# One core, three stacked blocks in float32: modulation sums by transposes, a joint compression of keys and values, a gMLP bias on VectorE and mLSTM maxima in float32r

## The chip, the core and the metric

The kernel runs on one NeuronCore of one Trainium2 chip. The metric is device time of one execution in microseconds (us). Matrix products run on TensorE (PE in the profile, its weight loads PEld), elementwise work on VectorE (DVE) and ScalarE (ACT), a little on GpSimd (POOL), and transfers are issued by SyncE (SP).

## The reference, cut to what matters

Three blocks follow each other on a sequence of 512 tokens of width 1024: an HGRN2 mixer with a gated convolution, a hybrid of gMLP, mLSTM and sparse attention (NSA) with an MLP, and a mixer of gated delta rule and RWKV-7 with a gated feed-forward part. The change touches four pieces of them:

```python
m = jax.nn.silu(cvec) @ w + b                      # modulation vectors, 1024 -> 3 or 6 times 1024

def compress_blocks(kv, pe, w1, w2):               # once for keys, once for values
    n_cmp = (S - CMP_BLOCK) // CMP_STRIDE + 1      # 31 blocks of 32 tokens, every 16
    idx = jnp.arange(n_cmp)[:, None] * CMP_STRIDE + jnp.arange(CMP_BLOCK)[None, :]
    blocks = kv[:, idx] + pe[:, None, :]
    blocks = blocks.transpose(0, 3, 1, 2, 4).reshape(B, G, n_cmp, CMP_BLOCK * dh)
    return jax.nn.gelu(blocks @ w1) @ w2

# gmlp_mixer: the bias is per group and token of a chunk
mixed = jnp.einsum('gts,bcsgd->bctgd', w, v) + bs.T[:, :, None]
return u * mixed.reshape(B, S, GM_W)

# mlstm_chunk_step: the running maximum m of each head and token enters two exponentials
s = jnp.einsum('bhtd,bhsd->bhts', q, k) * jnp.exp(d - m[..., None])
h = num / jnp.maximum(jnp.abs(den), jnp.exp(-m))[..., None]
```

## The kernel before, in words

Activations lie feature-major, 128 features on the partitions and 512 tokens along the row. Large products are done three times in float32r, with weights and activations split in a high and a low part (`mm3`, L320 to 327): high by high, high by low, low by high. `weight` (L303) loads 512 KB of weights into one of two raw buffers on SP's queue, ScalarE makes the high part (L310), VectorE the low part (L312). A projection is 24 such matmuls of 512 columns into one of three PSUM banks of tag "pj".

A planner in the framework orders the instructions: each has a priority (its place in the program, moved by `ahead`), and an engine is given what is ready by the planner's own durations. So instructions of one step lie between those of others, and the order on each engine is fixed before the run; at run time each engine takes its queue in that order.

The pieces that the change touches:

- `ada_later` (L483 to 501) makes 512 modulation values per step. VectorE sums eight weighted tiles of 128 by 512 into `ada_acc` (L492, L494). The sum over the 128 partitions is then taken by four matmuls with a quarter of `ada_acc` as the stationary operand and one column of ones as the moving one (L497), into a bank of tag "ad", of which there is one; VectorE adds the bias (L500). In float32 such a matmul has two records in the profile, so a step has eight. There are 32 steps: 12 in the loop over HGRN heads, 8 in the NSA steps, 12 in the MLP of block 2. The NSA steps use the same "ad" bank for gate projections.
- `small2` (L1119 to 1172) makes the mLSTM gate rows: scans on VectorE, a transpose (L1162), then eight ScalarE copies that put minus the running maximum and minus the total into rows 0 to 3 and 32 to 35 of `s_nmu` (L1170, L1171).
- `mlstm` (L1174) broadcasts, for each of four heads, one of those rows over 128 partitions by a matmul with a selecting matrix of four rows: twice before the scores (L1218, L1219; L1220 adds a mask to the second) and once after them (L1241). They are float32 of 512 columns, two records each.
- `nsa` (L1293 to 1321) first compresses keys, then values: project (24 matmuls), copy the result into `ns_st` in two shifts (L1302, L1303, ScalarE), 16 float32 matmuls with 64 columns of `ns_w` stationary and 3 times 31 strided columns of `ns_st` moving (L1306), a gelu, and a second small product (L1316, L1320).
- `gmlp` (L1476 to 1520): for each of four groups and four chunks, one product of 128 columns (L1513) and one product with a single row of ones that adds the bias (L1514) into the same bank; VectorE multiplies by `gm_u` (L1515).

Of the kernel before, what the change touches and what calls it, by code (L numbers as in the profile page):

```python
# [10 lines left out]
F32 = mybir.dt.float32  # L11
# [220 lines left out]
def dview(t, off, dims):  # L232

    return bass.AP(tensor=t.tensor, offset=t.offset + off, ap=[list(t.ap[0])] + [list(d) for d in dims])


class K:
# [245 lines left out]
    def ada_later(self, w, cond, groups, bias, out):  # L483

        def step(gi, grp):
# [9 lines left out]
            col = self.bank("ad", [P, 4])  # L495
            for b in range(4):
                nc.tensor.matmul(col[:, b:b + 1], acc[:, 128 * b:128 * b + 128], self.c("ones")[:, 0:1],  # L497
                                 start=True, stop=True)
            cs = slice(4 * gi, 4 * gi + 4)
            nc.vector.tensor_tensor(out[:, cs, 0], col, bias[:, cs], op=ALU.add)  # L500
# [618 lines left out]
    def small2(self, pl, pn):  # L1119
# [27 lines left out]
        L = pl.tile([P, S], F32, name="s2_L")  # L1147
# [17 lines left out]
        nn = pl.tile([36, S], F32, name="s2_nmu")  # L1165
# [6 lines left out]
        return gT, (acol, nmu, nm)  # L1172

    def mlstm(self, pl, pq, rows, ypair):  # L1174
# [4 lines left out]
        acol, nmu, nm = rows  # L1179
# [31 lines left out]
        for h in range(4):  # L1211
# [4 lines left out]
            sel, selm = [self.c("sel4")[a:a + 4, 128 * h:128 * h + 128] for a in (0, 32)]  # L1216
# [24 lines left out]
            mm(bm, selm, nm, start=True, stop=True)  # L1241
# [27 lines left out]
    def nsa(self, pn, gT, ypair, fill):  # L1269
# [18 lines left out]
        with tc_pool("x2_cmp") as pc:  # L1288
            for x, n in enumerate("kv"):
                st = pc.tile([P, 3, S], F32, name="ns_st", bufs=2)  # L1290
                pe = pn.tile([P, 16], F32, tag="pe", name="ns_pe")
                nc.sync.dma_start(pe, I["nsa_pe_" + n])
                w1 = pc.tile([P, 16, 64], F32, name="ns_w1", bufs=2)  # L1293
                nc.sync.dma_start(w1, I["nsa_phi_%s1" % n])
                w2 = pn.tile([64, 64], F32, tag="w2", name="ns_w2")
                nc.sync.dma_start(w2, I["nsa_phi_%s2" % n])
                nc.vector.memset(st[:, 2, :], 0.0)
                nc.vector.tensor_copy(dview(st[:, 2, :], 0, [[2, 16]]), pe)
                acc = self.proj_h(W[24 + x])
                for g in range(2):  # L1300
                    gs = slice(64 * g, 64 * g + 64)
                    nc.scalar.copy(st[0:64, g, :], acc[gs])  # L1302
                    nc.scalar.copy(st[64:128, g, 0:S - 1], acc[gs, 1:S])  # L1303
                hid = self.bank("mx", [64, 3, 31])
                for i in range(16):
                    mm(hid, w1[:, i, :], dview(st[:, :, :], 2 * i, [[S, 3], [16, 31]]), start=i == 0, stop=i == 15)  # L1306
                z, o = tmp("ns_z", [64, 2, 31]), tmp("ns_zo", [64, 2, 31])
# [886 lines left out]
```

## Time and profile before

| | |
|---|---|
| median of 3 runs (lowest, highest) | 3445.26 us (3436.17, 3450.95) |
| the profiled execution's own time | 3448.05 us |
| its span | 3446.3 us |
| PE, PEld, DVE, ACT busy share of the span | 96%, 77%, 70%, 52% |
| mean granted TensorE clock, share of full | 0.979 |
| HBM traffic over the span | 96 GB/s |

The profile is one execution. A row of the timeline gives the start in us from the span's start, the time to the end of the last instruction merged into it, engine, line, operation, the tile written and those read, shapes, and how many instructions; in brackets the idle time of the engine before it and what ended it. Because matmuls overlap, what one takes of TensorE is read from the distance of one start to the next, not from its duration. [...]

### The profile page before, as it was taken

How to read it: one execution, taken by the hardware profiler on the slowest of the kernel's cores; microseconds unless marked ns; L12 is line 12 of the kernel's file. 1: busy time of each engine (PE TensorE's matmuls, PEld its weight loads, DVE VectorE, ACT ScalarE, POOL GpSimd, SP SyncE). 2: the span in 40 equal slices, each digit the busy share in tenths (PEclk: the TensorE clock that was granted, in tenths of full speed). 3: DMA queues.
4: the chain of work that ended last, by engine and by line, in shares of the span. 5: the costliest groups of instructions: out<-in, count | busy, mean ns of one | idle time of the engine just before them, and what ended most of it. 6: DMA issues, size and time to landing. Idle time of an engine off the chain costs nothing.

```text
span 3446.3 us, 50617 instructions
## 1 busy us (share of the span) xinstructions
PE 3313.8 (96%) x20168; PEld 2647.7 (77%) x20168; DVE 2422.0 (70%) x3873; ACT 1808.1 (52%) x3020; POOL 123.6 (4%) x56
## 2 busy tenths in 40 slices
PE   7999999999799999999999999999999999999998
PEld 5888888888577777776787777878766767778886
DVE  7697767877789988667656456553777887655545
ACT  5566556566554556645445443333566665444434
POOL 0000000000032240000000000000000000000000
PEclk9999999999899999999999999999999999999999
DMA  6223333321122122334321235552311121322322
GB/s 226 87 95 97 103 95 104 100 85 60 44 68 68 62 69 97 123 101 126 107 84 59 84 120 180 179 164 98 105 57 52 52 66 62 120 89 95 98 93 85
DMA packets 113696, 332.43 MB, mean 96 GB/s; under 512 B 13170, under 2 KB 13810, under 8 KB 112819
## 3 DMA queue, kind: packets, MB, share of 16 engines
q1 hardware_dynamic: 113202, 328.41, 29.3%
q8 instruction: 158, 2.59, 0.3%
q0 software_dynamic: 256, 0.79, 0.1%
q14 instruction: 80, 0.65, 0.1%
HBM read 319.18 MB, written 9.96 MB: 96 GB/s over the span
## 4 chain that ended last, share of the span: by engine, by line
PE 76%; DVE 15%; ACT 4%; issue 2%; DMA 2%; SPq 0%; POOL 0%; DVEq 0%; ACTq 0%
PE ps_pj L326 19%; PE ps_pj L325 19%; PE ps_pj L327 19%; DVE w_lo L312 2%; DMA ada_raw<-ada_w 2%; PE ps_o L1444 1%; DVE iv_m L1817 1%; ACT w_hi L310 1%; PE ps_ad L497 1%; PE ps_mx L326 1%; DVE iv_xd L1818 1%; DVE cv_ul L318 1%; PE ps_mx L724 1%; DVE ada_acc L494 1%; PE ps_mx L327 1%
## 5 line engine op out<-in xcount | busy, mean ns | idle before, releaser
L325 PE MATMUL ps_pj<-hh,w_hi 128*128 128x512 f32 x2344 | 939.0, 402 | 20.0 <-ACT hh L397 18.9
L326 PE MATMUL ps_pj<-hl,w_hi 128*128 128x512 f32 x2344 | 934.0, 399 | 0.0
L327 PE MATMUL ps_pj<-hh,w_lo 128*128 128x512 f32 x2344 | 933.2, 399 | 0.0
L310 ACT CAST w_hi<-w_raw 128x1024 fp32r<-128x1024 f32 (+1 forms) x435 | 454.7, 1045 | 758.0 <-PE ps_pj L326 653.4
L312 DVE TENSOR_TENSOR w_lo<-w_raw,w_hi 128x1024 fp32r<-128x1024 f32 (+1 forms) x387 | 470.1, 1216 | 309.3 <-ACT w_hi L310 301.9
L325 PEld LDWEIGHTS ps_pj<-hh,w_hi 128*128 128x128 f32 x2344 | 445.5, 190 | 129.5 <-ACT hh L397 24.5
L326 PEld LDWEIGHTS ps_pj<-hl,w_hi 128*128 128x128 f32 x2344 | 445.3, 190 | 101.3 <-issue 11.8
L327 PEld LDWEIGHTS ps_pj<-hh,w_lo 128*128 128x128 f32 x2344 | 445.1, 190 | 100.8 <-issue 11.1
L494 DVE SCALAR_TENSOR_TENSOR ada_acc<-ada_raw,sv_t_c,ada_acc 128x512 f32<-128x512 f32 x224 | 167.3, 747 | 57.7 <-DMA ada_raw<-ada_w 56.3
L968 DVE SCALAR_TENSOR_TENSOR xT<-ps_pj,ad,xT 128x512 f32<-128x512 f32 x128 | 95.4, 748 | 153.6 <-PE ps_pj L327 153.0
L312 POOL TENSOR_TENSOR w_lo<-w_raw,w_hi 128x1024 fp32r<-128x1024 f32 x48 | 121.1, 2522 | 1176.0 <-ACT w_hi L310 1176.0
L910 DVE SCALAR_TENSOR_TENSOR ps_mx<-cv_ut,vec,ps_mx 128x448 f32<-128x448 f32 (+3 forms) x192 | 128.1, 668 | 1.9 <-PE ps_mx L327 1.0
L910 DVE SCALAR_TENSOR_TENSOR ps_ad<-cv_ut,vec,ps_ad 128x480 f32<-128x480 f32 (+2 forms) x192 | 128.4, 669 | 1.6 <-ACT ps_ad L899 0.5
L325 PE MATMUL ps_pj<-w_hi,hh 128*128 128x256 f32 x416 | 120.4, 290 | 0.8 <-ACT hh L397 0.7
L327 PE MATMUL ps_pj<-w_hi,hl 128*128 128x256 f32 x416 | 118.7, 287 | 2.5 <-DVE hl L398 2.5
L326 PE MATMUL ps_pj<-w_lo,hh 128*128 128x256 f32 x416 | 121.0, 292 | 0.0
L326 PE MATMUL ps_pj<-m_yl,w_hi 128*128 128x512 f32 x256 | 99.8, 390 | 0.0
L327 PE MATMUL ps_pj<-m_yh,w_lo 128*128 128x512 f32 x256 | 99.6, 389 | 0.0
L325 PE MATMUL ps_pj<-m_yh,w_hi 128*128 128x512 f32 x256 | 99.6, 389 | 0.0
L327 PEld LDWEIGHTS ps_pj<-w_hi,hl 128*128 128x128 f32 x416 | 80.7, 195 | 3.9 <-DVE hl L398 3.2
L325 PEld LDWEIGHTS ps_pj<-w_hi,hh 128*128 128x128 f32 x416 | 80.8, 194 | 3.1 <-issue 1.4
L326 PEld LDWEIGHTS ps_pj<-w_lo,hh 128*128 128x128 f32 x416 | 80.8, 194 | 1.9 <-issue 1.1
(783 smaller groups left out, 6430.2 us busy)
## 6 DMA issues: line engine op xcount, KB each, us to landing
ada_raw<-ada_w SPq DMA_DIRECT2D x288, 256.0 KB, 3.0
w_raw<-w_in SPq DMA_DIRECT2D x97, 512.0 KB, 3.7
w_raw<-hgrn_w_in SPq DMA_DIRECT2D x64, 512.0 KB, 3.7
w_raw<-w_mlp SPq DMA_DIRECT2D x64, 512.0 KB, 3.7
w_raw<-conv_w_in SPq DMA_DIRECT2D x48, 512.0 KB, 3.6
w_raw<-w_ffn_in SPq DMA_DIRECT2D x44, 512.0 KB, 3.5
w_raw<-hgrn_w_v SPq DMA_DIRECT2D x16, 512.0 KB, 3.7
w_raw<-hgrn_w_out SPq DMA_DIRECT2D x16, 512.0 KB, 3.7
```

The source lines that it names most:

```text
L310: nc.scalar.copy(hi, raw)
L312: (nc.gpsimd if self.on_pool else nc.vector).tensor_tensor(lo, raw, hi.bitcast(F32), op=ALU.subtract)
L318: self.nc.vector.tensor_tensor(lo, src, hi.bitcast(F32), op=ALU.subtract)
L325: mm(out, wh, xh, start=first, stop=False)
L326: mm(out, wh, xl, start=False, stop=False)
L327: mm(out, wl, xh, start=False, stop=last)
L494: nc.vector.scalar_tensor_tensor(acc, raw, cond[:, k:k + 1], acc, op0=ALU.mult, op1=ALU.add)
L497: nc.tensor.matmul(col[:, b:b + 1], acc[:, 128 * b:128 * b + 128], self.c("ones")[:, 0:1], start=True, stop=True)
L724: mm(up[:, 128 * j:128 * j + 128], kT[:, d, j, :], vx[:, j, hs], start=True, stop=True)
L910: stt(o, x, tap(j), o, op0=ALU.mult, op1=ALU.add)
L968: self.nc.vector.scalar_tensor_tensor(self.xT[:, m, :], acc, gate[:, m:m + 1], self.xT[:, m, :], op0=ALU.mult, op1=ALU.add)
L1444: mm(out[64 * g:64 * g + 64, 128 * s:], vt[:, s, 128 * b + 64 * g:128 * b + 64 * g + 64], pts[g][:, c:c + S - 128 * s], start=b == 0 and s ...
```

## The change

- The modulation sum: four transposes into a whole bank of 4 by 128 columns, a VectorE reduction over the 128 columns, and the bias added in place, instead of four matmuls with a column of ones.
- Compression: keys and values share one input tile `ns_st` of 2 by 3 by 512 and one weight tile `ns_w` whose 128 columns are 64 of keys and 64 of values. One run of 16 matmuls has 186 moving columns and computes both; the halves that mix keys with weights of values are not used. There is one gelu of 128 rows instead of two of 64.
- mLSTM: the rows are split in a float32r high and low part in one tile of 36 rows (a cleared tile is copied in first, on VectorE; ScalarE writes the high rows, VectorE the low rows), and the selecting matmul takes all 36 rows in float32r, one record each, with one column of a small tile repeated 128 times as the stationary operand. `s2_L` and the unsplit rows move to a pool of five rotating buffers.
- gMLP: the row of biases is loaded to all partitions, VectorE adds it to the product from PSUM (`gm_z`) and multiplies by `gm_u` in a second instruction. The matmuls with one row go.

```diff
--- before.py
+++ after.py
@@ -492,12 +492,12 @@
                     nc.vector.tensor_scalar(acc, raw, cond[:, k:k + 1], None, op0=ALU.mult)
                 else:
                     nc.vector.scalar_tensor_tensor(acc, raw, cond[:, k:k + 1], acc, op0=ALU.mult, op1=ALU.add)
-            col = self.bank("ad", [P, 4])
+            tr = self.bank("ad", [P, 4, P])
             for b in range(4):
-                nc.tensor.matmul(col[:, b:b + 1], acc[:, 128 * b:128 * b + 128], self.c("ones")[:, 0:1],
-                                 start=True, stop=True)
+                nc.tensor.transpose(tr[:, b, :], acc[:, 128 * b:128 * b + 128], self.c("ident"))
             cs = slice(4 * gi, 4 * gi + 4)
-            nc.vector.tensor_tensor(out[:, cs, 0], col, bias[:, cs], op=ALU.add)
+            nc.vector.tensor_reduce(out[:, cs, 0], tr, axis=mybir.AxisListType.X, op=ALU.add)
+            nc.vector.tensor_tensor(out[:, cs, 0], out[:, cs, 0], bias[:, cs], op=ALU.add)
         self.later += [lambda gi=gi, grp=grp: step(gi, grp) for gi, grp in enumerate(groups)]
 
     def take(self, n):
@@ -1144,7 +1144,7 @@
         self.logsig(f, f, e2)
         self.load_consts("b2m", pl, tag="wt", bufs=1)
 
-        L = pl.tile([P, S], F32, name="s2_L")
+        L = tmp("s2_L")
         nc.vector.tensor_tensor_scan(L, self.c("mask128"), f, 0.0, op0=ALU.mult, op1=ALU.add)
         G = e2
         nc.vector.memset(G[:, S - 1:S], 0.0)
@@ -1162,21 +1162,33 @@
             nc.tensor.transpose(tr[:, 128 * i:128 * i + 128], ig[:, 128 * i:128 * i + 128], self.c("ident"))
         acol = pl.tile([P, 4, 4, 4], F32, name="s2_acol")
         nc.scalar.copy(acol, tr.rearrange("p (a b c) -> p a b c", a=4, b=4)[:, :, :, 0:4])
-        nn = pl.tile([36, S], F32, name="s2_nmu")
+        nn = tmp("s2_nn", [36, S])
         nmu, nm = nn[0:4], nn[32:36]
         tt(L, L, mu, op=ALU.add)
         for j in range(4):
             cs = slice(128 * j, 128 * j + 128)
             nc.scalar.mul(nmu[:, cs], mu[32 * j:32 * j + 4, cs], -1.0)
             nc.scalar.mul(nm[:, cs], L[32 * j:32 * j + 4, cs], -1.0)
-        return gT, (acol, nmu, nm)
+
+        z = G[0:36]
+        nc.vector.memset(z, 0.0)
+        parts = []
+        for x, u, l in ((nmu, slice(0, 4), slice(32, 36)), (nm, slice(32, 36), slice(0, 4))):
+            r = pl.tile([36, S], F32R, name="s2_r%d" % len(parts))
+            nc.vector.tensor_copy(r, z)
+            nc.scalar.copy(r[u], x)
+            tt(r[l], x, r[u].bitcast(F32), op=ALU.subtract)
+            parts.append(r)
+        selr = pl.tile([36, 4], F32R, name="s2_sel")
+        nc.vector.tensor_copy(selr, dview(self.c("sel4")[0:36], 0, [[128, 4]]))
+        return gT, (acol, parts, selr)
 
     def mlstm(self, pl, pq, rows, ypair):
         nc, I = self.nc, self.I
         W = I["w_in_2"]
         tt, stt, mm = nc.vector.tensor_tensor, nc.vector.scalar_tensor_tensor, nc.tensor.matmul
         tmp = self.tmp
-        acol, nmu, nm = rows
+        acol, (nmu, nm), selr = rows
         ones, ident = self.c("ones"), self.c("ident")
         pads = []
         for i in range(2):
@@ -1213,7 +1225,7 @@
             hs = slice(128 * (h % 2), 128 * (h % 2) + 128)
             v = vs[h]
 
-            sel, selm = [self.c("sel4")[a:a + 4, 128 * h:128 * h + 128] for a in (0, 32)]
+            sel = selr[:, h:h + 1].to_broadcast([36, P])
             bo, bd = self.bank("mx"), self.bank("mx")
             mm(bo, sel, nmu, start=True, stop=True)
             mm(bd, sel, nmu, start=True, stop=False)
@@ -1238,7 +1250,7 @@
                 wi = wt[:, off[i]:off[i] + S - 128 * i]
                 mm(num[:, 128 * i:], v[:, i, hs], wi, start=i == 0, stop=i == 3)
             bm = self.bank("mx")
-            mm(bm, selm, nm, start=True, stop=True)
+            mm(bm, sel, nm, start=True, stop=True)
             d, m = td("ml_d"), td("ml_m")
             nc.scalar.activation(d, den, AF.Abs)
             nc.scalar.activation(m, bm, AF.Exp)
@@ -1286,39 +1298,39 @@
         cmp_k = [pn.tile([P, 2, 32], F32R, name="ns_ck%d" % g) for g in range(2)]
         cmp_v = pn.tile([31, 2, 64], F32, name="ns_cv")
         with tc_pool("x2_cmp") as pc:
+
+            st = pc.tile([P, 2, 3, S], F32, name="ns_st")
+            w1 = pc.tile([P, 16, 2, 64], F32, name="ns_w1")
+            w2 = pn.tile([P, 64], F32, tag="w2", name="ns_w2")
             for x, n in enumerate("kv"):
-                st = pc.tile([P, 3, S], F32, name="ns_st", bufs=2)
                 pe = pn.tile([P, 16], F32, tag="pe", name="ns_pe")
                 nc.sync.dma_start(pe, I["nsa_pe_" + n])
-                w1 = pc.tile([P, 16, 64], F32, name="ns_w1", bufs=2)
-                nc.sync.dma_start(w1, I["nsa_phi_%s1" % n])
-                w2 = pn.tile([64, 64], F32, tag="w2", name="ns_w2")
-                nc.sync.dma_start(w2, I["nsa_phi_%s2" % n])
-                nc.vector.memset(st[:, 2, :], 0.0)
-                nc.vector.tensor_copy(dview(st[:, 2, :], 0, [[2, 16]]), pe)
+                nc.sync.dma_start(w1[:, :, x, :], I["nsa_phi_%s1" % n])
+                nc.sync.dma_start(w2[half[x]], I["nsa_phi_%s2" % n])
+                nc.vector.memset(st[:, x, 2, :], 0.0)
+                nc.vector.tensor_copy(dview(st[:, x, 2, :], 0, [[2, 16]]), pe)
                 acc = self.proj_h(W[24 + x])
                 for g in range(2):
-                    gs = slice(64 * g, 64 * g + 64)
-                    nc.scalar.copy(st[0:64, g, :], acc[gs])
-                    nc.scalar.copy(st[64:128, g, 0:S - 1], acc[gs, 1:S])
-                hid = self.bank("mx", [64, 3, 31])
-                for i in range(16):
-                    mm(hid, w1[:, i, :], dview(st[:, :, :], 2 * i, [[S, 3], [16, 31]]), start=i == 0, stop=i == 15)
-                z, o = tmp("ns_z", [64, 2, 31]), tmp("ns_zo", [64, 2, 31])
-                pb = pn.tile([64, 1], F32, tag="pb", name="ns_pb")
-                nc.vector.tensor_copy(pb, hid[:, 2, 0:1])
-                nc.vector.tensor_scalar(z, hid[:, 0:2, :], pb, None, op0=ALU.add)
-                self.gelu(o, z, tmp, [64, 2, 31])
-                for g in range(2):
-                    if n == "k":
-                        c = self.bank("mx", [P, 32])
-                        nc.vector.memset(c[64 * g:64 * g + 64, 31:32], 0.0)
-                        mm(c[64 * g:64 * g + 64, 0:31], w2, o[:, g, :], start=True, stop=True)
-                        stack(cmp_k[g], c, g)
-                    else:
-                        c = self.bank("mx", [31, 64])
-                        mm(c, o[:, g, :], w2, start=True, stop=True)
-                        nc.vector.tensor_copy(cmp_v[:, g, :], c)
+                    nc.scalar.copy(st[0:64, x, g, :], acc[half[g]])
+                    nc.scalar.copy(st[64:128, x, g, 0:S - 1], acc[half[g], 1:S])
+            hid = self.bank("mx", [P, 6, 31])
+            for i in range(16):
+                mm(hid, w1[:, i, :, :].rearrange("p a b -> p (a b)"), dview(st[:, :, :, :], 2 * i, [[S, 6], [16, 31]]),
+                   start=i == 0, stop=i == 15)
+            z, o = tmp("ns_z", [P, 2, 31]), tmp("ns_zo", [P, 2, 31])
+            pb = pn.tile([P, 1], F32, tag="pb", name="ns_pb")
+            for x in range(2):
+                nc.vector.tensor_copy(pb[half[x]], hid[half[x], 3 * x + 2, 0:1])
+                nc.vector.tensor_scalar(z[half[x]], hid[half[x], 3 * x:3 * x + 2, :], pb[half[x]], None, op0=ALU.add)
+            self.gelu(o, z, tmp, [P, 2, 31])
+            for g in range(2):
+                c = self.bank("mx", [P, 32])
+                nc.vector.memset(c[half[g], 31:32], 0.0)
+                mm(c[half[g], 0:31], w2[half[0]], o[half[0], g, :], start=True, stop=True)
+                stack(cmp_k[g], c, g)
+                c = self.bank("mx", [31, 64])
+                mm(c, o[half[1], g, :], w2[half[1]], start=True, stop=True)
+                nc.vector.tensor_copy(cmp_v[:, g, :], c)
 
         ks = []
         for b in range(2):
@@ -1481,8 +1493,8 @@
         rows = pg.tile([P, 2, 512], F32, name="gm_rows")
         for r in range(2):
             nc.sync.dma_start(rows[:, r, :], I["gm_rows_2"][r:r + 1, :].partition_broadcast(P))
-        bs = pg.tile([1, 512], F32, name="gm_bs")
-        nc.sync.dma_start(bs, I["gm_rows_2"][2:3, :])
+        bs = pg.tile([P, 512], F32, name="gm_bs")
+        nc.sync.dma_start(bs, I["gm_rows_2"][2:3, :].partition_broadcast(P))
         ws = pg.tile([P, 4, P], F32, name="gm_ws")
         nc.sync.dma_start(ws, I["gm_ws_2"])
         tt(ws, ws, self.c("triu").unsqueeze(1).to_broadcast([P, 4, P]), op=ALU.mult)
@@ -1510,9 +1522,11 @@
             mixed = self.bank("mx")
             for c in range(4):
                 cs = slice(128 * c, 128 * c + 128)
-                mm(mixed[:, cs], v[:, c, 128 * g:128 * g + 128], ws[:, g, :], start=True, stop=False)
-                mm(mixed[:, cs], self.c("ones")[0:1, :], bs[:, 128 * g:128 * g + 128], start=False, stop=True)
-            tt(u, u, mixed, op=ALU.mult)
+                mm(mixed[:, cs], v[:, c, 128 * g:128 * g + 128], ws[:, g, :], start=True, stop=True)
+            z = tmp("gm_z", [P, 4, P])
+            tt(z, mixed.rearrange("p (c t) -> p c t", c=4),
+               bs[:, 128 * g:128 * g + 128].unsqueeze(1).to_broadcast([P, 4, P]), op=ALU.add)
+            tt(u, u, z.rearrange("p c t -> p (c t)"), op=ALU.mult)
             y = [pg.tile([P, S], F32R, name="gm_y%d%d" % (g, i)) for i in range(2)]
             self.split(y[0], y[1], u)
             ys.append(y)
```

## Rows read from the trace of the kernel before

**Rows 1.** The page's busy times, and the chain that ended last, by engine.
```profile
PE 3313.8 (96%) x20168; PEld 2647.7 (77%) x20168; DVE 2422.0 (70%) x3873; ACT 1808.1 (52%) x3020; POOL 123.6 (4%) x56
...
PE 76%; DVE 15%; ACT 4%; issue 2%; DMA 2%; SPq 0%; POOL 0%; DVEq 0%; ACTq 0%
```
**Rows 2.** Stretches: length, busy PE, PEld, DVE, ACT, POOL, clock, DMA share, GB/s.
```profile
120.00:760.00 640.00, 631.95 (x5359) 546.45 (x5358) 497.77 (x719) 380.35 (x573) 0.00 (x0) 1.00 0.31 98
1475.00:1680.00 205.00, 196.86 (x990) 143.99 (x989) 144.09 (x407) 99.24 (x238) 0.00 (x0) 0.93 0.39 122
1680.00:1970.00 290.00, 289.65 (x1308) 223.88 (x1307) 167.93 (x226) 147.22 (x250) 0.00 (x0) 0.98 0.23 77
2064.00:2320.00 256.00, 247.54 (x1107) 202.96 (x1106) 150.21 (x203) 92.24 (x125) 0.00 (x0) 0.98 0.55 175
```
**Rows 3.** PE timeline: an HGRN modulation sum, four transposes soon after.
```profile
173.84 0.95 PE L497 MATMUL ps_ad<-cst_g,ada_acc 128*128 128x1 f32 x8
174.65 0.49 PE L325 MATMUL ps_pj<-hh,w_hi 128*128 128x512 f32 x1
174.97 0.40 PE L326 MATMUL ps_pj<-hl,w_hi 128*128 128x512 f32 x1
175.21 0.40 PE L327 MATMUL ps_pj<-hh,w_lo 128*128 128x512 f32 x1
...
176.60 0.60 PE L682 MATMUL ps_mx<-cst_g,hg_kc 128*128 128x128 f32 x4
...
177.26 0.39 PE L325 MATMUL ps_pj<-hh,w_hi 128*128 128x512 f32 x1
```
**Rows 4.** PE timeline: a modulation sum of the NSA steps.
```profile
1540.36 1.81 PE L497 MATMUL ps_ad<-cst_g,ada_acc 128*128 128x1 f32 x8 [0.72 <-DVE ada_acc L494]
1542.43 0.80 PE L325 MATMUL ps_ad<-hh,w_hi 128*128 128x512 f32 x1 [0.25 <-DVE ad L500]
```
**Rows 5.** Groups by line and shape: the nearest reduction on DVE.
```profile
L2009 DVE TENSOR_REDUCE gd_rs<-gd_sq 128x8 f32<-128x512 f32 x4 | 2.7, 684 | 2.5 <-ACT gd_sq L2007 2.4
```
**Rows 6.** PE timeline: the two compressions; then their weight loads (by line).
```profile
1435.60 5.29 PE L1306 MATMUL ps_mx<-ns_st,ns_w 128*64 128x93 f32 x32
1440.81 0.50 PE L325 MATMUL ps_pj<-hh,w_hi 128*128 128x512 f32 x1
...
1441.71 5.29 PE L1306 MATMUL ps_mx<-ns_st,ns_w 128*64 128x93 f32 x32
...
L1306 PEld LDWEIGHTS ps_mx<-ns_st,ns_w x64: 132/153/154, 1435.6 to 1446.5; 128*64 128x64 f32 x64
```
**Rows 7.** ACT and DVE timelines beside the first compression.
```profile
1439.98 0.58 ACT L1303 COPY ns_st<-ps_pj 64x511 f32<-64x511 f32 x1
1440.59 1.05 ACT L310 CAST w_hi<-w_raw 128x1024 fp32r<-128x1024 f32 x1
...
1440.92 0.15 DVE L1309 COPY ns_pb<-ps_mx 64x1 f32<-64x1 f32 x1 [3.77 <-PE ps_mx L1306]
```
**Rows 8.** PE timeline: the selecting matmuls of the first mLSTM head.
```profile
1683.45 1.12 PE L1218 MATMUL ps_mx<-s_nmu,cst_b 4*128 4x512 f32 x2
...
1685.36 1.12 PE L1220 MATMUL ps_mx<-cst_b,cst_g 128*128 128x512 f32 x2
...
1701.45 1.12 PE L1241 MATMUL ps_mx<-s_nmu,cst_b 4*128 4x512 f32 x2
1702.50 0.50 PE L326 MATMUL ps_pj<-hl,w_hi 128*128 128x512 f32 x1
```
**Rows 9.** PE timeline: gMLP chunks; stretches after two of their blocks (columns as rows 2).
```profile
1821.24 0.49 PE L1513 MATMUL ps_mx<-gm_ws,gm_v 128*128 128x128 f32 x2
...
1822.07 0.49 PE L1513 MATMUL ps_mx<-gm_ws,gm_v 128*128 128x128 f32 x2
...
1824.00:1831.00 7.00, 7.00 (x19) 5.20 (x20) 4.66 (x8) 2.94 (x5) 0.00 (x0) 0.53 0.18 66
1838.00:1845.00 7.00, 7.00 (x15) 3.78 (x13) 3.37 (x6) 4.44 (x11) 0.00 (x0) 0.55 0.13 50
```

## Prediction

> **What bounds the kernel now.** First the page's busy times and the engines of the chain that ended last [rows 1]: TensorE is busy for 96% of the span and carries 76% of the chain, VectorE 70% and 15%. So a us taken off TensorE's queue is worth nearly a us, and a us added to VectorE some 0.15 us, an estimate from its share of the chain. Then the stretches in which the changed steps lie [rows 2]: in all four TensorE is busy for 96% or more and VectorE for 58 to 78%. In the stretch with mLSTM and gMLP TensorE has no idle time that the view shows, 289.65 of 290 us; in the HGRN heads it has 8 us of 640. Last the timelines of the single steps, where the distance between starts counts.
>
> **Modulation sums.** A sum takes from 173.84 to the L326 at 174.97, and one ordinary matmul of 0.23 us lies in that (the next one follows after 0.24 us): 1.13 - 0.23 = 0.90 us [rows 3]. Four transposes of the same size take from 176.60 to 177.26, again with one ordinary matmul in it: 0.66 - 0.23 = 0.43 us [rows 3]. A step gains 0.47 us. In the NSA steps four of the eight sums run at the half clock and take 1.81 us like the one shown [rows 4]; half as many records should take half, so 0.90 us each. Sum: 28 x 0.47 + 4 x 0.90 = 16.8 us off TensorE.
>
> VectorE gets one more instruction per step, a reduction of 512 columns, for which the nearest row is 0.68 us from SBUF [rows 5]; this one reads PSUM. 32 x 0.68 = 21.8 us, at 0.15 on the path 3.3 us. The bias add stays. What is queued behind the reduction on VectorE waits for the transposes as it waits for the four matmuls now. In NSA the next user of the one "ad" bank is a gate projection, which already waits 0.25 us for the add [rows 4]; there are three such places, and each gets the 0.68 us more, 2.0 us. Net gain 16.8 - 3.3 - 2.0 = 11.5 us. The ends: 16.8 if VectorE hides all, a loss of 5 if the whole 21.8 us came onto the path.
>
> **Compression.** The 64 records of L1306 become 32, and each has twice the columns. Now a record takes 5.21 / 32 = 0.163 us for 93 columns [rows 6], while a transpose with 128 columns takes 0.43 / 4 = 0.11 us [rows 3]: these columns are slow ones, or the weight load, 0.153 us for 64 columns, sets the pace [rows 6]. In the first case 186 columns take 0.33 us and nothing is gained: 32 x 0.33 = 10.4 us, as now. In the second 32 records take 0.16 to 0.19 us each, up to 6 us, a gain of 4 to 5 us. I take the first, since L497 loads 128 columns every 0.11 us (0.90 / 8) [rows 3], so a load of 64 need not take 0.16.
>
> [...]
>
> There is a cost besides. The first run, of keys, starts at 1435.60, while ScalarE still copies the values into `ns_st` until 1440.56, and the next projection's weights are only cast from 1440.59 [rows 7]. So 5 us of the two runs lie now where TensorE has nothing else. The merged run needs all copies, and two more ScalarE copies of `small2` (0.58 us each, as the copy shown) stand ahead of them: it starts near 1441.7 and takes 10.4 us, to 1452.1; now both runs end at 1447.0 [rows 6]. That costs 5.1 us. VectorE's additions in `small2` (a clearing, two copies, two subtractions, a small copy, some 3 us at no more than 0.68 us each [rows 5]) fit into the 3.77 us for which it idles before the first result [rows 7]; without that cover they would delay the copies' readers by as much. The ends: 5 us gained if the load sets the pace and the planner puts the copies first, 8 us lost if the pause also lowers the clock for a stretch like that after the gMLP blocks, at 0.53 for 7 us, 3.3 us [rows 9]. The saved gelu (seven small instructions) is off TensorE's path: nothing. The loads of `ns_w` now land in runs of 64 columns; the first projections of the block cover them, so I set them at nothing; uncovered, a load would hold the run by its own time.
>
> **mLSTM rows.** Per head, L1218 and L1219 take from 1683.45 to 1685.36, 1.91 us, and L1241 from 1701.45 to 1702.50, 1.05 us: 2.96 us [rows 8]. In float32r each has one record; at the pace of L326 they take 3 x 0.23 = 0.69 us [rows 3]. Two float32 records of 512 columns should take 2 x 4 x 0.11 = 0.86 us by the transposes' pace [rows 3]; L1241's pair takes 1.05, so I put 0.1 us on each switch of the array from 128 rows to 4 and back (an estimate), and keep two switches at each of two places, 0.4 us, for 36 rows. So 1.1 us per head, a gain of 1.86, for four heads 7.4 us. The ends: 4.5 us if float32r with 36 rows runs only at the float32 pace of one pass, 9 us if the switches go too.
>
> **gMLP bias.** A chunk takes from 1821.24 to 1822.07, 0.83 us [rows 9], and there are 16 chunks, 13.3 us, and somewhat more since two of them run at the half clock: 14 us. Left are two records of 128 columns each, 0.11 us [rows 3]: 16 x 0.22 = 3.5 us. The gain is 10.5 us in a stretch with no idle TensorE time. VectorE adds four instructions of 0.68 us, 2.7 us, at 0.15 on the path 0.4 us. The load of biases to all partitions grows, with its issue on SP far ahead of its use: nothing.
>
> [...] Each fall costs about 3.2 us (7 x 0.47 or 0.45), of which some 1.5 us are already in the sums above. With blocks a quarter as long the falls may stay away: between 0 and 5 us more, I take 2.5.
>
> **The sum.** 11.5 - 5.1 + 7.4 + 10.1 + 2.5 = 26.4 us. The profiled execution took 3448.05 us (its span and 1.75 us around it), so 3421.6; that execution is 2.8 us above the median of the three runs, from which it would be 3418.9. I predict 3420 us. Unpriced is the order: the planner works with changed durations and may place steps elsewhere. The nearest row is the 8 us of TensorE idle time that it now leaves in the HGRN heads [rows 2]; I allow 8 us either way and take 0.
>
> **Rivals.**
> 1. *The freed time turns into waits.* TensorE takes its queue in order, and a step that comes sooner may find its VectorE or DMA input not ready; L497 waits for `ada_acc` already [rows 4]. If half of the 34.7 us that leave TensorE (16.8, 7.4, 10.5) is lost, the rest is 17.4 - 5.7 (VectorE) - 5.1 = 6.6 us: 3441 us. For it: VectorE is at 78% in the HGRN heads. Against: the mLSTM and gMLP stretch shows no idle TensorE [rows 2]. Chance 0.23.
> 2. *VectorE is the bound where its work grows.* Then TensorE's savings count nothing and each added us counts whole: 21.8 + 2.7 + 3.0 in `small2`, and the 5.1 of the compression: 32.6 us slower, 3480 us. The place is the HGRN loop and the MLP, and it decides from where VectorE's busy time in a stretch reaches TensorE's; it is 498 against 632 us in the one, 150 against 248 in the other [rows 2]. Chance 0.06.
> 3. *Transposes let the clock fall.* If after each of the 24 sums that lie in dense streams the clock went to half for a stretch as in rows 9, that were 24 x 3.2 = 77 us: 3497 us. Against it, the HGRN heads hold transposes like L682 in every head, and the granted clock there is 1.00 over 640 us [rows 2, 3]. Chance 0.03. [...]
> 4. *The compression gains instead of losing*, by its better end of 5 us: 3410 us. Chance 0.08.
> 5. *The selector does not run in one pass of float32r* and the mLSTM part gives nothing: 3427 us. Chance 0.03.
>
> **How the numbers follow.** The forecast has 0.57, with a range of its own from 3404 (all ends of gain: 16.8 + 7.4 + 10.1 + 5 + 5 = 44) to 3434 (the planner's 8 us and a costly compression against it). A measurement of this kernel tells about 0.5% from no change, 17 us, so faster means below 3428. Faster: nine tenths of the forecast, rivals 4 and 5: 0.62. Same: the rest of the forecast and rival 1: 0.29. Slower: rivals 2 and 3: 0.09. The range that should hold 8 in 10 takes in rivals 1 and 4 and half of the planner's 8 us on either side: 3400 to 3445.
>
> **What would show it.** Right: eight records of L497 become four transposes in 0.43 us; 32 records of L1306 about 0.33 us apart, starting after 1441 less what was gained before; one record of 0.23 us for each selecting matmul; no records of one row in gMLP, and a granted clock of 1.00 after its blocks; the HGRN stretch some 5 us shorter, mLSTM with gMLP some 20 us, the MLP stretch 5 us. Wrong: idle time on TensorE ahead of L497's successor that ends with VectorE, a clock below 1.00 after transposes, or a stretch that changed by more than its own parts.

## The result and the profile after

The changed kernel takes 3416.4 us (median of 7 runs, 3410.9 to 3432.7), the kernel before 3444.5 us beside it (7 runs, 3436.2 to 3451.0). The ratio is 0.9919, with a 95% interval from 0.9901 to 0.9936: 28 us faster, between 22 and 34. The forecast was 3420 us, a gain of 26.4 us. Its total was right; of its terms some were right and others cancelled. Span times mean granted clock, an estimate of the time without the clock's falls, is 3373.5 us in the median of 31 runs of before and 3354.7 us in that of the changed kernel's seven: some 19 of the 28 us are work and waits, and the rest came with the clock.

The profiled execution took 3417.6 us with a span of 3415.8 us. The page's busy times and its chain, to compare with [rows 1]:

```profile
PE 3269.4 (96%) x19964; PEld 2610.9 (76%) x19964; DVE 2442.1 (71%) x3911; ACT 1805.3 (53%) x3017; POOL 123.8 (4%) x56
...
PE 72%; DVE 16%; ACT 6%; DMA 4%; issue 2%; SPq 0%; POOL 0%; DVEq 0%; ACTq 0%
```

TensorE's busy time fell by 44.4 us and the span by 30.5. To see where, I cut both traces at the same events: the first and the last copy into `hg_dec` (HGRN heads), the first instruction that writes `ns_mx` and the first that writes `ml_wt` (NSA), from there to the first that writes `m_r` (mLSTM with gMLP), and from there to the last of `m_r` (MLP). The windows of before, in this order (length, busy PE, PEld, DVE, ACT, POOL, clock, DMA share, GB/s):

```profile
99.30:883.50 784.20, 774.39 (x6556) 666.58 (x6555) 609.13 (x880) 470.27 (x708) 0.00 (x0) 1.00 0.29 91
1480.20:1685.60 205.40, 197.31 (x988) 143.54 (x987) 145.40 (x410) 99.42 (x240) 0.00 (x0) 0.93 0.39 123
1685.60:2083.70 398.10, 394.77 (x1761) 309.48 (x1761) 234.71 (x311) 193.96 (x315) 0.00 (x0) 0.98 0.25 85
2083.70:2398.00 314.30, 308.82 (x1385) 254.58 (x1384) 161.06 (x206) 111.95 (x151) 0.00 (x0) 0.99 0.50 159
```

and of after:

```profile
98.00:885.90 787.90, 771.80 (x6508) 658.56 (x6507) 615.66 (x892) 469.90 (x708) 0.00 (x0) 1.00 0.29 91
1482.80:1681.90 199.10, 188.87 (x961) 136.97 (x960) 149.04 (x418) 99.05 (x239) 0.00 (x0) 0.94 0.42 128
1681.90:2062.60 380.70, 374.46 (x1708) 298.65 (x1707) 236.58 (x316) 192.24 (x314) 0.00 (x0) 0.99 0.28 89
2062.60:2370.00 307.40, 300.32 (x1340) 246.75 (x1339) 167.42 (x217) 112.02 (x151) 0.00 (x0) 1.00 0.51 163
```

| stretch | before | after | difference | forecast, by the same terms |
|---|---|---|---|---|
| HGRN heads | 784.2 | 787.9 | +3.7 | -4.4 (12 x 0.47, less 8.2 x 0.15) |
| compression (first read of `s_sg` to first `ns_mx`) | 55.9 | 57.7 | +1.8 | +5.1 |
| NSA | 205.4 | 199.1 | -6.3 | -2.7 |
| mLSTM with gMLP | 398.1 | 380.7 | -17.4 | -20.0 |
| MLP | 314.3 | 307.4 | -6.9 | -4.4 |

The five sum to -25.1 against -26.4. That these are so near is luck: taken by size, the five differences from the forecast add up to 20 us. The rest of the program, which is unchanged, gave another 5 us in this execution. In the experiments below whose code for a stretch is that of before, the HGRN heads took 783.5 to 784.3 us, NSA 204.2 to 207.6 and the MLP 310.2 to 314.3: a difference of 4 us stands out in the heads and not in the MLP. mLSTM with gMLP took 397.4 to 399.0 us where its code is that of before, but 391.3 in one execution (`a_col`), at a mean clock of 1.00 instead of 0.98.

The single steps, in the timeline of after (start, us, engine, line; in brackets the idle time before and what ended it):

```profile
1443.24 1.51 PE L1318 MATMUL ps_mx<-ns_st,ns_w 128*128 128x186 f32 x4 [1.51 <-ACT ns_st L1315]
...
1679.09 0.49 PE L1230 MATMUL ps_mx<-s_r,s_sel 36*128 36x512 f32 x1
1679.42 0.39 PE L1231 MATMUL ps_mx<-s_r,s_sel 36*128 36x512 f32 x1
1679.75 1.13 PE L1232 MATMUL ps_mx<-cst_b,cst_g 128*128 128x512 f32 x2
...
1697.84 0.49 PE L1253 MATMUL ps_mx<-s_r,s_sel 36*128 36x512 f32 x1
1698.26 0.50 PE L326 MATMUL ps_pj<-hl,w_hi 128*128 128x512 f32 x1
...
1802.91 0.71 PE L1525 MATMUL ps_mx<-gm_ws,gm_v 128*128 128x128 f32 x4
...
1820.33 0.50 PE L325 MATMUL ps_pj<-hh,w_hi 128*128 128x512 f32 x1 [2.32 <-DVE gm_u L985]
```

The compression's matmuls by the view of one tile (duration least/median/most in ns, first and last start), and two stretches of the clock (columns as above):

```profile
L1318 PE MATMUL ps_mx<-ns_st,ns_w x32: 490/492/562, 1443.2 to 1453.1; 128*128 128x186 f32 x32
```
```profile
1442.00:1449.00 7.00, 5.76 (x19) 4.90 (x20) 3.75 (x5) 3.15 (x4) 0.00 (x0) 0.76 0.34 103
...
1821.00:1828.00 7.00, 7.00 (x17) 4.93 (x16) 3.65 (x7) 4.37 (x11) 0.00 (x0) 0.52 0.16 64
```

The selecting matmuls take 0.33 + 0.33 + 0.42 = 1.08 us per head (2.96 before, [rows 8]; 1.1 forecast). No one-row matmuls stand between the gMLP products. The merged compression has 32 records 9.9 / 31 = 0.32 us apart and starts after 1.51 us of idle time. One fall of the clock behind gMLP is left (mean 0.52 over the 7 us shown) where there were two [rows 9]. Behind the last gMLP product TensorE now idles for 2.32 us, until VectorE writes `gm_u`.

### The profile page after: what moved, and what is told of

Read it like the earlier page. It is cut to its first block, busy times and chain, and to the rows that moved or that the text cites. A ratio compares the mean times of both kernels' runs of the same rounds, so it can differ in the third digit from the quotient of the medians.

```text
span 3415.8 us, 50235 instructions
## 1 busy us (share of the span) xinstructions
PE 3269.4 (96%) x19964; PEld 2610.9 (76%) x19964; DVE 2442.1 (71%) x3911; ACT 1805.3 (53%) x3017; POOL 123.8 (4%) x56
## 4 chain that ended last, share of the span: by engine, by line
PE 72%; DVE 16%; ACT 6%; DMA 4%; issue 2%; SPq 0%; POOL 0%; DVEq 0%; ACTq 0%
PE ps_pj L326 18%; PE ps_pj L325 18%; PE ps_pj L327 18%; DMA ada_raw<-ada_w 3%; DVE w_lo L312 2%; ACT w_hi L310 1%; DVE ada_acc L494 1%; DVE iv_m L1831 1%; PE ps_o L1456 1%; PE ps_mx L326 1%; DVE cv_ul L318 1%; DVE iv_xd L1832 1%; PE ps_mx L724 1%; PE ps_mx L327 1%; PE ps_mx L325 1%
```

## The experiments

### Each part alone

Four kernels, each the kernel before with one part of the diff above: `a_sums` its first hunk, `m_rows` the hunks in `small2` and `mlstm`, `c_comp` the hunk in `nsa`, `g_bias` the two in `gmlp`.

```diff
a_sums: @@ ada_later     +nc.tensor.transpose, +tensor_reduce
m_rows: @@ small2, mlstm +s_r, +s_sel, float32r selecting matmuls
c_comp: @@ nsa           +one run of 16 matmuls for keys and values
g_bias: @@ gmlp          -one-row matmuls, +gm_z
```

> The modulation sums alone, all else as before. Theory 1, each step is worth what it takes off TensorE less 0.15 of VectorE's work: 11.5 us faster than before, about 3433 us, with the HGRN heads 5 us shorter. Theory 2, in the HGRN heads the time taken off TensorE (12 steps, 10.4 to 4.9 us in the changed kernel) comes back as waits, because VectorE has 0.68 us more per step there: the HGRN heads end no earlier than before or up to 2.5 us later, the NSA and MLP steps gain their 8 us, together 6 to 9 us faster, about 3437 us.

> The joint compression alone. Forecast: 32 records about 0.31 us apart and a start after 1441 us, the first scores 5 us later than before, about 5 us slower in all. Rival: the planner fills the time ahead of the run with the next projection, as it did in the changed kernel, and only 1 to 2 us are lost. Second rival: 5 us faster, if the records come at the pace of the weight load, 0.16 us.

> The mLSTM rows alone. Forecast: 1.9 us per head off TensorE in a stretch where TensorE has no idle time, 7.4 us faster, about 3437 us, three selecting records of 0.33 to 0.42 us per head. Rival: the time turns into waits for VectorE, less than 3 us faster.

> The gMLP bias alone. Forecast: 10.5 us less of TensorE's time and one or two stretches at the half clock less, 10 to 13 us faster, about 3433 us. Rival: the product must now wait for two VectorE instructions instead of one and the half of it comes back, 5 us faster; the clock falls as often as before.

| kernel | ratio to before (95%) | its own stretch, before to this |
|---|---|---|
| `a_sums` | 0.9951 (0.9935 to 0.9968) | heads 784.2 to 788.4, NSA 205.4 to 199.9, MLP 314.3 to 305.4 |
| `c_comp` | 0.9996 (0.9976 to 1.0016) | compression 55.9 to 57.4 |
| `m_rows` | 0.9967 (0.9950 to 0.9984) | mLSTM with gMLP 398.1 to 390.4 |
| `g_bias` | 0.9970 (0.9946 to 0.9993) | mLSTM with gMLP 398.1 to 388.0 |

The mLSTM rows give 7.7 us and the gMLP bias 10.1 us in their stretch, together 17.8, and the whole change 17.4: most of what leaves TensorE's queue in this stretch, which had little idle time [rows 2], is gained. Not all is: TensorE's idle time in it grows from 3.3 to 6.2 us (the windows above), most of it in the one wait for `gm_u`. This wait of 2.3 us stands in all five kernels with the gMLP change and in none of the others. The compression costs 1.5 us and not 5.1: the rival of `c_comp` was right. The modulation sums gain, but not in the heads: there theory 2 of `a_sums` was right, though its whole gain of 17 us (11 to 22) is nearer to theory 1. The reason that theory 2 gave, VectorE's reduction, was tested next.

By their ratios the four parts add up to 40 us, the whole change to 28. Each of the ratios is known to within 6 to 8 us, so this difference is not clear of noise.

### Why the heads gain nothing

```diff
a_col (a_sums, VectorE takes one column):
-tensor_reduce(out[:, cs, 0], tr, axis=X, op=add)
-tensor_tensor(out[:, cs, 0], out[:, cs, 0], bias[:, cs], op=add)
+tensor_tensor(out[:, cs, 0], tr[:, :, 0], bias[:, cs], op=add)
x_dve (before, one reduction more):
+tensor_reduce(junk, acc.rearrange("p (a b) -> p a b", a=4), axis=X, op=add)
a_act (a_sums, reduced on ScalarE):
-tensor_reduce(out[:, cs, 0], tr, axis=X, op=add)
+for b in range(4): activation(tr[:, b, :], tr[:, b, :], Copy, accum_out=out[:, 4 * gi + b, 0:1])
hyb (the whole change; sums 1 to 12 as before):
+if self.nsum <= 12: matmul(col[:, b:b + 1], acc[...], ones[:, 0:1]) ...
```

> The modulation sums alone, but VectorE takes one column of each transposed quarter instead of the sum of its 128 (this leaves out the summing over partitions): TensorE does the same as in the full change, VectorE does as little as before. If VectorE's 0.68 us per step is what ate the gain in the HGRN heads (there 4.2 us slower from head 0 to head 15), the heads are now 4 to 6 us shorter than before and the whole about 20 us faster, 3428 us. Rival: the planner's changed order alone makes the waits; the heads stay 2 to 4 us longer than before and the whole is 12 to 16 us faster, as with the reduction.

> The kernel before with one more VectorE reduction of 512 columns (0.68 us, from ada_acc into an unused tile) ahead of each bias add; TensorE does what it did. If VectorE's work is on the path in the HGRN heads, these become 4 to 10 us longer (12 steps, up to 0.68 us each, 8.2 us) and the rest little longer: 5 to 12 us slower in all. If VectorE hides it, as the 0.15 of the forecast has it, the heads become 1.2 us longer and the whole 3.3 us. Rival, only the order matters: a change of either sign of up to 4 us in the heads.

> The modulation sums alone, with the reduction on ScalarE: four activations of 128 columns that add up their row, instead of one VectorE reduction; everything is computed. If VectorE's reduction eats the gain, the heads are 2 to 6 us shorter than before (ScalarE has 59% busy in them) and the whole is 16 to 22 us faster, 3427 us. Rival: ScalarE's four instructions stand in the way of the casts of weights, on which VectorE waits for some 100 us in these heads, and the heads are as long as with the reduction on VectorE, 4 us longer than before.

> The whole change, but the 12 modulation sums of the HGRN heads keep the matmuls with a column of ones. Theory, VectorE's reductions are paid for in the heads: these are as before (785 us from head 0 to head 15, where the changed kernel takes 3.7 us more), NSA, mLSTM, gMLP and MLP keep their gains, and the whole is about 3.5 us faster than the changed kernel, 32 us faster than before, 3413 us. Rival: a different order elsewhere gives it back, no difference from the changed kernel.

| kernel | heads | NSA (clock) | MLP | ratio to before (95%) |
|---|---|---|---|---|
| before | 784.2 | 205.4 (0.93) | 314.3 | 1 |
| `a_sums` | 788.4 | 199.9 (0.94) | 305.4 | 0.9951 (0.9935 to 0.9968) |
| `a_col` | 787.5 | 192.3 (0.99) | 306.6 | 0.9926 (0.9903 to 0.9950) |
| `x_dve` | 784.5 | 206.1 (0.93) | 314.2 | 1.0000 (0.9976 to 1.0024) |
| `a_act` | 789.5 | 193.7 (0.98) | 306.0 | 0.9936 (0.9911 to 0.9961) |
| `hyb` | 783.5 | 200.0 (0.94) | 309.3 | 0.9926 (0.9902 to 0.9950) |
| `x_ord` | 787.2 | 201.9 (0.95) | 308.3 | 1.0004 (0.9986 to 1.0023) |

My theory fell. Without the reduction the heads are still 3.3 us longer than before (`a_col`; with it 4.2, `a_sums`), with it on ScalarE 5.3 us longer, and one more reduction on VectorE costs 0.3 us (`x_dve`, where the planner also moved some instructions). So VectorE hides most of it (0.3 us out of 12 reductions of 0.68), as the forecast had it. `hyb` shows only the place: with the old sums in the heads, where TensorE and ScalarE then have exactly the order of before, these are as before, 4.4 us shorter than in the changed kernel. Its whole time can't be told from that of the changed kernel.

What was left was the order. For a test of it alone, `x_ord` makes the sums by matmuls again, with 64 columns of ones:

```diff
x_ord (from a_col):
-nc.tensor.transpose(tr[:, b, :], acc[:, 128 * b:128 * b + 128], ident)
+nc.tensor.matmul(tr[:, b, 0:64], acc[:, 128 * b:128 * b + 128], ones[:, 0:64], start=True, stop=True)
```

All engines' instructions stand in the same order in `x_ord` and `a_col` (but for some TensorE records of block 3 that start a few ns apart); only TensorE's work per sum differs. Both differ from before in many places.

> Modulation sums by matmuls again, but with 64 columns of ones (all 64 columns of the result alike, VectorE takes the first): the planner takes such a matmul for as long as a transpose, and every engine gets exactly the order of the kernel that takes one column of each transpose; on the chip the sums have two records each, as before (12 groups in the heads at some 0.90 us where the transposes take 0.43). Theory, the planner's order costs the gain: from head 0 to head 15 the kernel before takes 784.2 us, the transposes in this order 787.5; with the old TensorE work in this order the heads take 787.5 + 5.5 = 793 us, 9 us more than before. Rival, the time of the sums is not on the path in the heads: 788 us or less, as with the transposes.

The heads take 787.2 us with the long sums and 787.5 with the short ones: in the same order TensorE's 0.45 us per sum is worth nothing. And 787.2 against 784.2 with the same work is what the order costs. The rival was right. Transposes in the order of before were not run, so what they would be worth there is open. The timelines of one place show how the time is given back; first `x_ord`, then `a_col`:

```profile
322.31 1.00 PE L497 MATMUL ps_ad<-cst_g,ada_acc 128*128 128x64 f32 x8
323.12 0.37 PE L325 MATMUL ps_pj<-w_hi,hh 128*128 128x256 f32 x1
...
326.67 0.65 PE L681 MATMUL ps_mx<-cst_g,hg_kc 128*128 128x128 f32 x4 [0.31 <-ACT hg_kc L677]
```
```profile
321.84 0.60 PE L497 MATMUL ps_ad<-cst_g,ada_acc 128*128 128x128 f32 x4
322.19 0.36 PE L325 MATMUL ps_pj<-w_hi,hh 128*128 128x256 f32 x1
...
326.64 0.65 PE L681 MATMUL ps_mx<-cst_g,hg_kc 128*128 128x128 f32 x4 [1.22 <-ACT hg_kc L677]
```

The sum ends 0.93 us earlier in `a_col` (0.45 of its own, 0.40 because the heads begin that much earlier there, and 0.08 gained before), and the transposes of `hg_kc` start at the same time, since ScalarE has `hg_kc` no sooner: 1.22 us idle instead of 0.31. What holds `hg_kc` is a load. VectorE waits for a tile of modulation weights until the same time in both, again `x_ord` and then `a_col`, and the steps to `hg_kc` stand behind it in the queues of VectorE and ScalarE:

```profile
316.87 0.75 DVE L494 SCALAR_TENSOR_TENSOR ada_acc<-ada_raw,sv_t_c,ada_acc 128x512 f32<-128x512 f32 x1 [0.47 <-DMA ada_raw<-ada_w]
```
```profile
316.85 0.75 DVE L494 SCALAR_TENSOR_TENSOR ada_acc<-ada_raw,sv_t_c,ada_acc 128x512 f32<-128x512 f32 x1 [0.93 <-DMA ada_raw<-ada_w]
```

The waits of TensorE over the heads, before, `x_ord` and `a_col` (sum in us, times, longest):

```profile
PE ps_o L787 <- DVE hg_a L780: 7.4, 13, 0.8
...
PE ps_mx L682 <- ACT hg_kc L678: 0.3, 1, 0.3
```
```profile
PE ps_o L786 <- DVE hg_a L779: 7.7, 13, 1.1
PE ps_mx L765 <- DVE hg_qd L760: 1.9, 5, 0.5
PE ps_mx L681 <- ACT hg_kc L677: 1.3, 2, 1.0
```
```profile
PE ps_o L786 <- DVE hg_a L779: 7.8, 13, 1.1
PE ps_mx L765 <- DVE hg_qd L760: 2.8, 5, 0.8
PE ps_mx L681 <- ACT hg_kc L677: 2.5, 3, 1.2
```

The order of `x_ord` adds waits for `hg_qd` and `hg_kc` (2.9 us), and these grow by 2.1 us when the sums get shorter. The windows of the two kernels' heads:

```profile
98.30:885.50 787.20, 774.56 (x6556) 665.55 (x6555) 609.78 (x879) 470.20 (x708) 0.00 (x0) 1.00 0.29 91
```
```profile
97.90:885.40 787.50, 771.60 (x6508) 658.69 (x6507) 609.01 (x879) 470.09 (x708) 0.00 (x0) 1.00 0.29 91
```

TensorE's idle time grows from 12.6 to 15.9 us; the other 2 us of the 5.4 saved show in no wait, only in longer distances between starts. As the order is the same, the two traces can be lined up record by record. Of the 5.4 us, 2.9 come back at the transposes of `hg_kc`, 0.9 at `hg_qd`, 0.6 at `hg_yl` and the rest in small pieces. `hg_kc` is late at eight places, and at six of them no wait shows: in `x_ord` the transposes start 0.31 us after ScalarE has finished `hg_kc`, in `a_col` 0.05 us after. So 0.26 of the 0.45 us were a lead that TensorE could use up, and 0.18 are lost; the start comes 0.42 us behind the one ahead of it (174.46 to 174.88) instead of 0.24 (175.29 to 175.53), which the duration of the matmul ahead, 0.39, covers. At `hg_qd` the sum stands inside the wait: VectorE's steps to it begin at a product that TensorE starts before the sum (445.77 and 448.11 in `x_ord`), so a shorter sum only lengthens the wait.

So the heads are not bound by TensorE's queue alone, though it is busy for 98.7% of them in before: at those places it arrives just when its operand does, or with less lead than the sums save.

The last run asked whether it is VectorE's amount of work that makes these operands late:

```diff
thin (the whole change):
-                else:
+                elif k == 1:
                     nc.vector.scalar_tensor_tensor(acc, raw, cond[:, k:k + 1], acc, ...)
```

> The whole change, with two instead of eight weighted tiles added up per modulation step on VectorE (six of eight terms of each modulation sum are left out; their loads stay): some 4.4 us less of VectorE's time per step, ahead of the point where the sums are taken. If the time that the transposes free is taken back by waits for VectorE's work (ada_acc in the MLP, 5.4 to 6.2 us of waiting; hg_kc, hg_qd and hg_yl in the HGRN heads), the heads become 5 to 12 us shorter than in the changed kernel (787.9 us from head 0 to head 15) and the MLP 4 to 6 us: 12 to 25 us faster than the changed kernel. Rival: the waits stand at places that VectorE's amount of work doesn't move, and the heads stay within 2 us; only the MLP's wait for ada_acc goes, 4 us faster.

The whole is 0.9878 of before (0.9849 to 0.9906). Its heads and its MLP:

```profile
98.20:883.00 784.80, 770.35 (x6508) 659.56 (x6507) 572.25 (x819) 471.39 (x708) 0.00 (x0) 1.00 0.29 91
2050.60:2352.10 301.50, 299.81 (x1342) 247.88 (x1340) 123.77 (x152) 112.14 (x151) 0.00 (x0) 1.00 0.51 164
```

With 43.4 us less of VectorE's work the heads are 3.1 us shorter than after, between the two expectations and near the rival's, and still 0.6 us longer than before: how full VectorE is makes at most a small part. That the length of the chain of steps makes the rest is argued, not shown. The order changed here too, and with the additions VectorE's waits for their loads went as well (10.0 us in the heads of after, none in `thin`), so it is not settled which link that is. In the MLP it is otherwise: there TensorE waits at the sum for `ada_acc`, in before and after

```profile
PE ps_ad L497 <- DVE ada_acc L494: 5.4, 6, 1.6
```
```profile
PE ps_ad L497 <- DVE ada_acc L494: 7.1, 8, 1.8
```

and in `thin` this wait is gone and the stretch 5.9 us shorter. `ada_acc` in turn waits for the loads of its eight tiles (35.8 us of VectorE's idle time there in after, by the same view).

### NSA: the sums and the clock

`a_col` and `a_act` gain 12 to 13 us in NSA, with a mean clock of 0.98 to 0.99 against 0.93. Length times clock is 187 to 192 us in all of these kernels (before 205.4 x 0.93 = 191, `a_col` 192.3 x 0.99 = 190): most of what differs there is the clock. In the timeline of after the sum at 1541 is taken at the half clock (0.50 of full from 1541.05 to 1542.16), and TensorE pauses ahead of it and behind it:

```profile
1541.05 1.11 PE L497 MATMUL ps_ad<-cst_g,ada_acc 128*128 128x128 f32 x4 [0.72 <-DVE ada_acc L494]
1542.94 0.80 PE L325 MATMUL ps_ad<-hh,w_hi 128*128 128x512 f32 x1 [0.78 <-DVE ad L499]
```

The first pause was there before, the second was 0.25 us [rows 4]. The waits at these sums, for `ada_acc` and for the result in "ad" (a wait of 1.4 us for `x_merged`, in all of them, not counted), add up to 2.5 us before (0.93), 3.8 after (0.94), 1.5 in `x_ord` (0.95), 1.8 in `a_col` (0.99), 1.6 in `a_act` (0.98) and none in `thin` (0.99). With long sums the clock stays low (0.93 and 0.95), with short ones it is high (0.98 to 0.99) only where the pauses are short too (1.8 us or less; 0.94 with 3.8 us): `x_ord` and `a_col`, in one order, differ by the length alone and by 9.6 us. Their other runs agree: the mean granted clock of the whole is 0.974 to 0.982 in the ten of `x_ord` and 0.983 to 0.987 in the eight of `a_col`. Which of the two sets the fall at each sum isn't settled. So I put the old sums in the heads and the reduction on ScalarE together:

```diff
best (hyb, with the reduction of a_act):
-tensor_reduce(out[:, cs, 0], tr, axis=X, op=add)
+for b in range(4): activation(tr[:, b, :], tr[:, b, :], Copy, accum_out=out[:, 4 * gi + b, 0:1])
```

> The whole change, with two of the findings: the 12 sums of the HGRN heads keep the matmuls with a column of ones, and the 20 sums after them are reduced on ScalarE instead of VectorE. Theory, in the NSA steps the reduction holds the one bank that the gate projections wait for, and the pauses bring stretches at the half clock: HGRN heads as before (3.7 us less than in the changed kernel), NSA 4 to 6 us shorter than in the changed kernel, the rest alike: 8 to 10 us faster than the changed kernel, near 3408 us. Rival: the order changes again and each gain is given back elsewhere, within 3 us of the changed kernel.

```profile
1537.39 0.66 PE L506 MATMUL ps_ad<-cst_g,ada_acc 128*128 128x128 f32 x4
1537.81 1.18 PE L1424 MATMUL ps_pj<-ns_k,ns_q 128*128 128x512 f32 x4
1539.71 0.50 PE L325 MATMUL ps_ad<-hh,w_hi 128*128 128x512 f32 x1 [0.73 <-ACT ps_ad L508]
```

In its profile the same sum runs at full clock (1.00 from 1534 to 1548), the heads are as before (784.2), NSA takes 196.5 us at 0.97, and the span is 7 us shorter than after (3408.8). But over five rounds it takes 0.9923 of before (0.9907 to 0.9940), no other than the changed kernel. The gain that one profile shows is not confirmed.

### The compression's columns

```diff
c_stride1 (from c_comp):
-dview(st[:, :, :, :], 2 * i, [[S, 6], [16, 31]])
+dview(st[:, :, :, :], 2 * i, [[S, 6], [1, 31]])
```

> The joint compression alone, reading 31 neighbouring columns instead of every 16th one (other columns, so the compressed keys and values are left out as such). If the stride makes the columns slow, the 32 records fall from 0.31 to 0.11 to 0.16 us each and the run from 10 to 4 to 5 us. Rival, the pace is that of 186 float32 columns at any stride: 0.31 us and 10 us as before.

The rows of the tile, `c_comp` and `c_stride1`:

```profile
L1306 PE MATMUL ps_mx<-ns_st,ns_w x32: 490/492/561, 1437.4 to 1447.2; 128*128 128x186 f32 x32
```
```profile
L1306 PE MATMUL ps_mx<-ns_st,ns_w x32: 318/324/425, 1440.2 to 1445.3; 128*128 128x186 f32 x32
```

A record takes 9.8 / 31 = 0.316 us with every 16th column and 5.1 / 31 = 0.165 us with neighbours. The stride doubles it, and the weight load of 128 columns is no bound at 0.165 us.

## Why the prediction was right, step by step

**What bounds the kernel.** "A us taken off TensorE's queue is worth nearly a us" held for most of mLSTM with gMLP, where little idle time showed, and failed in the heads. There the 10 us of idle time, in some 17 short waits, were read as small change. They mark places where TensorE has no lead over its operands, so it can't win there, but they are only part of the sign: 13 of them are for `hg_a`, which stay as they are, and most of what was given back went at `hg_kc`, where before shows one wait of 0.3 us. A lead that is shorter than the saving shows in no wait: at six places of `hg_kc` it was 0.31 us against 0.45.

**Modulation sums.** The prices of the step were right: four transposes in 0.42 us (`best`, 1537.39 to 1537.81) for 0.43, and the reduction 0.68 us (7.5 us for 11 in `a_sums`). The forecast's sum for 32 steps, 11.5 us, came out as 4.2 lost in the heads, 5.5 gained in NSA and 8.9 in the MLP (`a_sums`): 10.2, by errors that cancel. The failed step is the heads: -4.4 forecast, +3.7 measured, of which some 3.0 is the order (by `x_ord`, whose order is near that of after), while TensorE's saving of 5.4 was given back whole. That is rival 1 in one stretch: it reckoned with half of the saving lost, and all went. The 8 us for the order, allowed either way, covered the rest. In the MLP the unchanged code varies by 4 us, so of the 6.9 there 3 to 7 are the change's.

**The wait for the "ad" bank.** Three waits of 0.25 us became three of 0.78 us (0.8 to 2.4 us): 1.6 us for the 2.0 forecast. What the forecast missed is that the clock in this stretch changes with the length of the sums (0.95 in `x_ord`, 0.99 in `a_col`), and as it seems with their pauses.

**Compression.** Right: no gain from fewer records, since the stride sets the pace (0.316 us a record with every 16th column, 0.165 with neighbours). The term that was mis-sized is the start: 5.1 us forecast, 1.8 measured. The run started at 1443.2, later than forecast, but the planner put the next projection's matmuls into most of the time ahead of it, and TensorE idled for 1.5 us. The feared fall of the clock came in after (mean 0.76 over the 7 us shown), and not in `c_comp`, where the same stretch has 1.00.

**mLSTM rows.** 1.08 us per head for 1.1, and 7.7 us for 7.4 in `m_rows`. The added steps on VectorE and ScalarE cost at most 0.5 us: ahead of the compression TensorE waits 1.4 us for `s_ig` in `m_rows`, 0.9 before.

**gMLP bias and clock.** 10.1 + 2.5 forecast, 10.1 measured in `g_bias` with the clock's part in it: of two falls one stays. The last pair of terms was 2.5 us too high. No run shows the 2.5 us, an estimate from the two stretches of [rows 9], by itself; what the runs show is one fall left, in after 6.8 us long at 0.50. The matmuls came out as forecast: the 64 records take 13.9 us of TensorE's queue before, and 32 records at 0.11 us are 3.5. The mis-sized term is VectorE's part, set at 0.4 us: TensorE's new wait for `gm_u` is 2.3 us. Its chain runs from a gMLP product over the added `gm_z` (1813.27 in after) and ScalarE's steps to the `gm_u` of the next block (1819.59). Whether the 0.69 us of `gm_z` or the planner's order makes more of it is open. The fall that stays begins in after 0.6 us behind this wait (1820.33 and 1820.96), and the mean clock of the stretch is 0.99 there, in `g_bias` and in `best`; `hyb` has the wait and no fall (1.00), and `a_col`, with the old gMLP, has neither fall (1.00), so a fall there is not tied to one cause.

**The other rivals.** VectorE as the bound (3480 us) falls by the result, and in the heads by `x_dve`. That transposes among dense matmuls pull the clock down is not seen: the heads hold 48 more of them at a mean clock of 1.00. A stretch of transposes alone was not tried.

## What to carry to other kernels

Before you price a matmul at its full worth, look at when the operands of TensorE's next few microseconds are ready: where it already waits for one, even for 0.3 us, what is saved ahead of that place can be given back there (a wait of 0.31 us for `hg_kc` became one of 1.22), and where an operand is ready only shortly before its use, so can all of the saving beyond that lead (0.18 of 0.45 us, behind a lead of 0.26). In a kernel whose order a planner makes, a changed step also changes the order everywhere; an instruction of other cost that the planner holds for equal separates the two effects. A sum of stretches that comes out right can hide errors of opposite sign, so compare stretch by stretch, and know how much an unchanged stretch varies between profiles.

## What the runs showed of the hardware

The clock fell for long in code that nobody touched. `m_rows` differs from before only in block 2, but in its profile a stretch of block 3 runs at a mean clock of 0.83, and its span came out 5 us longer than before although it is faster by 0.3% over its runs; first `m_rows`, then before at the same place:

```profile
2700.00:2800.00 100.00, 96.56 (x937) 72.56 (x935) 71.25 (x140) 53.05 (x110) 0.00 (x0) 0.83 0.15 48
```
```profile
2714.00:2814.00 100.00, 96.07 (x995) 71.11 (x994) 85.55 (x175) 62.70 (x128) 0.00 (x0) 1.00 0.16 52
```
